# A hybrid decoder layer on one core: half-array products queued side by side, the first tiles multiplied by feature halves, a new order in the mixer

## The chip, the cores and the metric

One core of a Trainium2 chip runs one launch of the whole layer. The metric is the device time of that launch in microseconds (us), the median of several runs. The engines are TensorE (PE in the profile; PEld is its load of weights, which overlaps PE), VectorE (DVE), ScalarE (ACT), GpSimd (POOL) and SyncE (SP), whose queue issues nearly all DMAs here.

## The reference

All arithmetic is float32, with 512 tokens of 1024 features:

```python
h = swiglu(rms_norm(x, ffn1_pre_norm), w_gate, w_up, w_down)       # hidden width 2816
x = x + 0.5 * rms_norm(h, ffn1_post_norm)
u = rms_norm(x, mix_pre_norm)                                      # then u @ w_in, split in columns
o_nsa = g0 * o_cmp + g1 * o_sel + g2 * o_win                       # sparse attention: 8 heads of 64 in 2 groups
o_dn  = rms_norm(gated_delta_rule(q, k, v, decay, beta)) * silu(z) # gated DeltaNet: 4 heads of 128
o_mem = memory_cross_attention(mem_q, mem)                         # 4 heads of 128, 256 memory tokens
merged = sum(sigmoid(u @ w_branch_gate[br]) * (o[br] @ w_branch[br]) for br in range(3))
x = x + rms_norm(merged @ w_out, mix_post_norm)
h = swiglu(rms_norm(x, ffn2_pre_norm), w_gate, w_up, w_down)
x = x + 0.5 * rms_norm(h, ffn2_post_norm)
```

Two inner parts matter here. The compressed keys and values of the sparse attention come from a small network, `silu(flat @ w1) @ w2`, over blocks of 32 tokens (`flat` is 2048 wide, `w1` is 2048 x 256, one for keys and one for values). And each attention branch ends in the product of probabilities and values.

## The kernel before

Large products run with three matmuls for one: each operand is split into a high part of reduced precision (fp32r) and the rest, and high x high, low x high and high x low are summed (`mm3`, L117 to L119). `wload` (L105 to L109) brings a weight tile of 128 x 512 by a DMA on SP, ScalarE makes the high part, and VectorE (or, for every n-th tile of a task that says so, GpSimd) the low part. The tiles go round a small ring of buffers (tag `wraw`). Small products run in plain float32, where each matmul shows as two records in the trace.

A planner sets the order of the work. `tasks` (L1122) walks a list of short names and emits each task's instructions in that order. `off` raises the priority of a task's instructions by so many places. A scheduler then lays out each engine's queue from these priorities and a model of when operands are ready; on the chip each queue runs in order. `order(later, earlier)` tells the scheduler to place one instruction behind another, with no semaphore of its own. The lists and numbers are in the table `PRM` (L37): `order_s` for the start, `order0` for the first down-projection, `order` for DeltaNet and compression, `order2` for sparse attention, memory attention and merging, `order3` for the output projection.

**Start.** Eight bf16 matmuls on zeros run first. The order of the tasks is

```
t00 w10 w00 y t01 t02 w01 t03 w11 R0 F000 x F101 n F200 t10 t11 t12 t13 c F110 B F211 F011
```

`t0k` transposes two of the eight feature tiles of the first 256 tokens; `y` loads the second half of those tokens' features (the first half is loaded ahead of the list); `x` loads the other 256 tokens; `w10` loads half of the first up weights, `w00` half of the first gate weights; `F f i` multiplies hidden tile f for token half i: 48 matmuls of 256 columns, 24 for the gate and 24 for the up part, each over all 8 feature tiles.

**Compression (tasks p0 to p7, `cmp_hid`, L928).** Each of the 8 calls loads two weight tiles of 256 KB, one for keys and one for values, from the shared ring, and makes 4 products, which alternate between keys (array columns and PSUM partitions 0 to 63) and values (64 to 127). In the trace the result is `phid`, the line L940.

**Sparse attention.** For head i, branch br and group g, task `S` makes scores and softmax (L1042 to L1051), `P` transposes the probabilities tile by tile (`nsa_pt`, L1062) and copies them out, and `V` multiplies with the values (`nsa_pv`, L1074): 8 products per call, for g = 0 in array columns 0 to 63 and for g = 1 in 64 to 127, of 512, 384, 256 and 128 columns. There are 8 calls. `M br j` are the merge's tiles, 36 matmuls of 512 columns each. Others that are named below: `c` convolution of DeltaNet (projection, then `cacc`), `h` its transposes and norms, `k`, `l` its small products (`pkk`), `b`, `e`, `d` the inverse of its triangular blocks (`pt`, `px`, `pxt`), `s` its states, `o` its output, `q` the query projections, `x` the input of compression, `K` the keys.

Of the kernel before, what the change touches and what calls it, by code (L numbers as in the profile page):

```python
# [36 lines left out]
PRM = {'order': ['i', 'a', 'w', 'c01', 'h01', 'r0', 'c00', 'c10', 'c02', 'l0', 'h00', 'h02', 'c12', 'k0', 'h10', 'c22', 'c11', 'h12', 'h11', 'h22', 'r1', 'k1', 'l1', 'b0', 'c21', 'z', 'h21', 'e0', 'c20', 'r2', 'h20', 'c32', 'l2', 'c31', 'd00', 'h31', 'k2', 'r3', 'd01', 'l3', 'b1', 'd02', 'x0', 's00', 'e1', 'd10', 'c30', 'h32', 'x1', 'd11', 'h30', 's01', 's02', 's03', 'q0', 'q3', 'p0', 'o0', 'p1', 'p2', 'p3', 'k3', 'd12', 's10', 'p4', 'q1', 'p5', 's11', 'p6', 'p7', 's12', 's13', 'o1', 'q2', 'f'], 'dma': {'l': 'sync', 'b': 'sync', 'd': 'scalar', 'c': 'sync', 'r': 'sync'}, 'off': {'b0': 300, 'h31': 400, 'r1': 50, 'h32': 50, 'h11': 200, 'h12': 200, 'd10': 100, 'A01': 100, 'A10': 100, 'A11': 100, 'A20': 400, 'A31': 100, 'A21': 20, 'x0': 20, 'x1': 20, 'L': 200, 'S310': 400, 'S001': 20, 'S311': 400, 'A30': 100, 'r0': 400, 'd02': 20, 's11': 100, 'V20': 400, 'l3': 100, 'q1': 20, 'f': 400, 'l1': 20, 'h20': 100, 'h22': 100, 'r3': 50, 'P010': 50, 'y': 100, 'h02': 50, 'S101': 20, 'A00': 100, 'Q0': 50, 'Q1': 200, 'Q2': 50, 'Q3': 50, 'P110': 400, 'V31': 50, 'd01': 200, 'o0': 400, 'p0': 50, 'p1': 50, 'p2': 50, 'p4': 50, 'p5': 20, 'p6': 50, 'p7': 50, 'b1': 200, 'h01': 100, 'M15': 20, 'P201': 400, 'e0': 100, 'e1': 100, 'o1': 20, 'q0': 50, 'q2': 20, 'h21': 20, 'd11': 50, 'p3': 50, 'U0': 100, 's13': 50, 'c11': 20, 's00': 200, 'P011': 400, 'M14': 200, 'c20': 50, 'k2': 20, 'M03': 20}, 'ph': 'e', 'po': 'ss', 'xpd': (0, 1, 2), 'order2': ['K1', 'K0', 'B', 'M10', 'Q0', 'C0', 'Q1', 'S000', 'C3', 'S001', 'P001', 'P000', 'C1', 'S010', 'C2', 'S011', 'V00', 'P010', 'Q2', 'S101', 'S100', 'P011', 'S110', 'V01', 'P100', 'W0', 'P101', 'S111', 'Q3', 'V10', 'P110', 'M12', 'S200', 'P111', 'V11', 'P200', 'S210', 'M14', 'S201', 'M15', 'P201', 'S211', 'W1', 'V20', 'P211', 'P210', 'V21', 'S301', 'S300', 'W2', 'P301', 'S311', 'M11', 'P300', 'L', 'M13', 'S310', 'G0', 'V30', 'P310', 'M16', 'G2', 'P311', 'M17', 'V31', 'W3', 'A00', 'M00', 'A01', 'G1', 'U0', 'M05', 'A10', 'A11', 'G3', 'A30', 'U1', 'A31', 'U3', 'M03', 'M06', 'A20', 'A21', 'U2', 'M07', 'M22', 'M20', 'M02', 'M24', 'M27', 'M21', 'M23', 'M01', 'M04', 'M26', 'M25'], 'order0': ['d0', 'p0', 'n0', 't0', 'd1', 'k2', 'k0', 'p2', 'p3', 'v', 'k3', 'n1', 'k1', 't1'], 'order3': ['s3', 's7', 's2', 's6', 's1', 's5', 's0', 's4', 'd00', 'd01', 'd11', 'g', 'p0', 'n0', 't0', 'd10', 'p1', 'n1'], 't3': (('mm', 'r'), ('e', 's')), 'pool': {'W2': 2, 's13': 3, 'k0': 0, 'k1': 0, 'k2': 0, 'k3': 2, 'p3': 1, 'C0': 1, 'C1': 0, 'C2': 0, 'C3': 2, 'S310': 0, 'L': 3, 'd11': 3, 'p0': 1, 'p1': 1, 'p2': 1, 'p4': 2, 'p5': 1, 'p6': 1, 'p7': 1, 'S311': 0, 'h01': 0, 'h00': 2, 'h02': 0, 'h10': 0, 'h11': 0, 'h12': 0, 'h22': 0, 'h21': 0, 'h20': 0, 'h31': 0, 'h30': 3, 'h32': 0, 'i': 2, 'P011': 2, 'c21': 0, 'd01': 2, 'S000': 0, 'S001': 0, 'S010': 0, 'S011': 0, 'S100': 0, 'S101': 0, 'S110': 0, 'S111': 0, 'S200': 0, 'S201': 0, 'S210': 0, 'S211': 0, 'S300': 0, 'S301': 0, 'M24': 2, 'G2': 2, 'A01': 0, 'M10': 1, 'M15': 2, 'M12': 2, 'M14': 2, 'M13': 2, 'M17': 2, 'M11': 2, 'M16': 2, 'M23': 0, 'M27': 3, 'M01': 2, 'M00': 2, 'M03': 0, 'M07': 2, 'M06': 1, 'M22': 2, 'M04': 2, 'M20': 2, 'M26': 3, 'M02': 0, 'M21': 2, 'M25': 2, 'M05': 2, 'c11': 1, 'o1': 3, 'P000': 2, 'P001': 1, 'P010': 2, 'P100': 2, 'P101': 2, 'P110': 2, 'P111': 2, 'P200': 2, 'P201': 2, 'P210': 2, 'P211': 2, 'P301': 0, 'P300': 2, 'P310': 2, 'P311': 2, 'c12': 0, 'b1': 1, 'x0': 0, 'x1': 0, 'V21': 0, 'c30': 0, 'c01': 0, 'c02': 0, 'c00': 0, 'c10': 0, 'c22': 0, 'c20': 0, 'c31': 0, 'c32': 0, 's01': 3, 'A31': 0, 'd12': 0, 'y': 2, 'G0': 2, 'G1': 2, 'G3': 0, 'U3': 0, 'W3': 2, 'r1': 2, 's12': 3, 'U2': 0, 'Q0': 2, 'Q1': 2, 'Q2': 2, 'Q3': 1, 's00': 3, 's02': 2, 's03': 3, 's10': 2, 's11': 3, 'e1': 2, 'd00': 1, 'U0': 0, 'U1': 0, 'l2': 0, 'd02': 2, 'K1': 3, 'V11': 0, 'V00': 2}, 'pool3': {'d00': 3, 'd01': 3, 'd10': 3, 'd11': 0, 'p1': 2, 't1': 3, 't0': 3, 's5': 2, 's7': 2, 's1': 2, 's0': 2, 's3': 2, 's6': 2, 's2': 2, 's4': 2, 'q0': 1}, 'pool0': {}, 'off0': {'p3': 20, 'n1': 50, 'd0': 200, 'k2': 400, 'k1': 400}, 'off3': {'s1': 20, 's5': 200, 'g': 200, 't0': 400, 'd10': 200, 'p0': 200}, 'tt': ('e', 's'), 'order_s': ['t00', 'w10', 'w00', 'y', 't01', 't02', 'w01', 't03', 'w11', 'R0', 'F000', 'x', 'F101', 'n', 'F200', 't10', 't11', 't12', 't13', 'c', 'F110', 'B', 'F211', 'F011'], 't0': ('e', 's'), 'rs': ((0, 0), (0, 0)), 'ra': (1, 1), 'warm': 8, 'pools': {'F000': 0, 'F101': 0, 'F200': 0, 'F011': 0, 'F110': 0, 'F211': 0, 'w10': 0, 'w11': 0, 't00': 0, 't01': 0, 't02': 0, 't03': 0, 't13': 0, 't10': 0, 't11': 0, 't12': 0, 'w00': 0, 'w01': 0}, 'ptc': 'vvs', 'cva': 'v', 'offs': {'t13': 100, 'R1': 400, 't03': 20, 'w10': 200}, 'vnc': 's', 'sp3': 0, 'hsc': 'vv', 'sf2': 2, 'psc': 'vvvv', 'sp1': 0, 'vbs': 'v', 't1c': 'vs', 'sgv': 256}  # L37


class Body:  # L40
# [172 lines left out]
    def scale(self, eng, out, src, r):  # L213
        if eng == "s":
            self.nc.scalar.activation(out, src, AF.Copy, scale=r)
        else:
            (self.nc.gpsimd if eng == "g" else self.nc.vector).tensor_scalar(out, src, r, None, op0=OP.mult)
# [709 lines left out]
    def cmp_hid(self, c, Xs, d):  # L927

        nc = self.nc
        if c == 0:  # L930
            d["ph"] = self.bank(PRM.get("ph", "e"), "phid")[:, :256]
        w1 = []
        for which in range(2):
            w = self.wp.tile([P, 2, 256], F32, tag="wraw", name="w1", bufs=self.WB[0])
            nc.sync.dma_start(w, self.a["cmp_w1"][which, c])
            w1.append(w)
        for k in range(2):
            m = 2 * c + k
            for which in range(2):
                nc.tensor.matmul(d["ph"][64 * which : 64 * which + 64], Xs[which][:, m].rearrange("p g c -> p (g c)"),  # L940
                                 w1[which][:, k], start=m == 0, stop=m == 15)
# [89 lines left out]
    def nsa_soft(self, i, g, br, A, K, tb, sg, ap_):  # L1031
# [16 lines left out]
        for qb in range(TB):  # L1048
            n = P * (qb + 1)
            pm = Pm[:, self.OFF[qb] : self.OFF[qb] + n]  # L1050
            self.scale(PRM.get("psc", "vvvv")[qb], pm, pm, sm[:, qb : qb + 1])  # L1051
        return Pm

    def nsa_pt(self, Pm, ap_):
        nc, v, te = self.nc, self.nc.vector, self.nc.tensor
        PT = ap_.tile([P, 1280], F32, tag="PT", name="PT", bufs=2)
        for bank, kbs in enumerate(((0,), (1, 3), (2,))):
            pt = self.bank("s", "ppt")
            o = 0
# [8 lines left out]
    def nsa_pv(self, i, br, po, pts, vt):
        te = self.nc.tensor
        col = (0, 512, 1024, 896)  # L1070
        for kb in range(TB):
            n = SEQ - kb * P
            for g in range(2):
                te.matmul(po[64 * g : 64 * g + 64, kb * P :], vt[:, kb, br * P + 64 * g : br * P + 64 * g + 64],  # L1074
                          pts[g][:, col[kb] : col[kb] + n], start=br == 0 and kb == 0, stop=False, skip_group_check=True)
# [51 lines left out]
    def run(self):  # L1127
# [3 lines left out]
        with tc.tile_pool(name="f1", bufs=1) as fp, contextlib.ExitStack() as x1:  # L1131
# [384 lines left out]
```

## Time and profile before

| | |
|---|---|
| median of 3 runs (lowest, highest) | 1361.38 us (1360.89, 1362.07) |
| the profiled execution's own time | 1360.6 us |
| its span, first to last instruction | 1358.8 us |
| mean granted clock of TensorE | 0.995 |
| DMA traffic | 178.32 MB, mean 131 GB/s |
| matmul records on PE | 7839 |

The stages lie so in the span: the first feed-forward block to about 345 us, DeltaNet and compression from there to some 640, sparse attention and the merge to some 985, the output projection and the second feed-forward block after that.

In a row of the timeline stand the start and the duration in us, engine, line, operation, output and inputs, the shape (rows*columns of the array, then the output), the number of records, and in brackets the idle time before it and what ended it. Matmuls are pipelined: a record's duration runs past the start of the next one, so what an instruction costs the queue is the distance between starts. In a table by stretch, each engine has its busy time and, in brackets, its number of instructions. A row of waits has who waited for what, the total, how often, and the longest.

### The profile page before, as it was taken

Reading aid. Unit: us, or ns where it says so; the run is one execution under the profiler, and the core shown is the slowest. Engines: PE = TensorE matmul, PEld = TensorE weight load, DVE = VectorE, ACT = ScalarE, POOL = GpSimd, SP = SyncE. Lnnn points to the kernel's source line nnn. Section 1 sums busy time; section 2 is a strip of 40 time slices with the busy share of each in tenths; the row PEclk is TensorE's granted clock in tenths of the full one; section 3 lists DMA queues with packets and bytes.
Section 4 is the critical chain, followed back from the end, with each engine's and each line's share of the span. In section 5 each row is a group of like instructions: output and inputs, shape, how many; then the busy total and the mean of one; then the engine's idle time right before and its main releaser. Section 6 shows DMA issues by size and latency. Waiting matters only on the chain.

```text
span 1358.8 us, 21802 instructions
## 1 busy us (share of the span) xinstructions
PE 1330.2 (98%) x7839; PEld 1128.1 (83%) x7839; DVE 899.9 (66%) x1802; ACT 717.7 (53%) x1538; POOL 142.3 (10%) x129
## 2 busy tenths in 40 slices
PE   8999999999999989999999999999999999999997
PEld 7889999788797778787767777788878899998886
DVE  6897876765768775745887323322688778766775
ACT  6566664765655543316655234333576566646652
POOL 0020000000011322003111112323200000000000
PEclk8999999999999999999999999999999999999999
DMA  7543331586664341423111222533744433317773
GB/s 246 194 149 118 100 119 32 178 255 184 210 187 131 83 124 41 126 95 120 52 47 48 78 62 68 189 95 92 257 139 140 135 122 98 121 33 255 199 223 106
DMA packets 107453, 178.32 MB, mean 131 GB/s; under 512 B 18908, under 2 KB 28496, under 8 KB 107344
## 3 DMA queue, kind: packets, MB, share of 16 engines
q1 hardware_dynamic: 107056, 176.67, 41.9%
q8 instruction: 61, 1.00, 0.3%
q14 instruction: 48, 0.39, 0.1%
q10 hardware_dynamic: 288, 0.26, 0.1%
HBM read 166.84 MB, written 10.01 MB: 130 GB/s over the span
## 4 chain that ended last, share of the span: by engine, by line
PE 88%; DVE 5%; ACT 2%; DMA 2%; issue 1%; POOL 0%; SPq 0%; ACTq 0%; DVEq 0%; POOLq 0%
PE smm L429 10%; PE pfm L117 7%; PE pfm L118 7%; PE pfm L119 7%; PE se L429 7%; PE ss L429 3%; PE po L1074 2%; PE ps L1042 2%; PE acc_e L118 2%; PE acc_e L119 2%; PE acc_e L117 2%; PE sr L429 2%; PE acc_s L119 1%; PE acc_s L117 1%; PE acc_s L118 1%; PE so L429 1%
## 5 line engine op out<-in xcount | busy, mean ns | idle before, releaser
L106 ACT CAST whi<-wraw 128x512 fp32r<-128x512 f32 (+1 forms) x314 | 189.8, 614 | 181.4 <-PE pfm L119 65.1
L109 DVE TENSOR_TENSOR wlo<-wraw,whi 128x512 fp32r<-128x512 f32 (+1 forms) x268 | 183.9, 694 | 125.3 <-ACT whi L106 118.2
L117 PE MATMUL pfm<-xth,whi 128*128 128x512 f32 x384 | 154.5, 405 | 3.0 <-DVE cacc L635 3.0
L118 PE MATMUL pfm<-xth,wlo 128*128 128x512 f32 x384 | 154.2, 405 | 1.0 <-POOL wlo L109 1.0
L119 PE MATMUL pfm<-xtl,whi 128*128 128x512 f32 x384 | 154.5, 405 | 0.0
L117 PEld LDWEIGHTS pfm<-xth,whi 128*128 128x128 f32 x384 | 72.4, 189 | 21.0 <-issue 5.2
L119 PEld LDWEIGHTS pfm<-xtl,whi 128*128 128x128 f32 x384 | 72.4, 188 | 16.3 <-issue 2.0
L118 PEld LDWEIGHTS pfm<-xth,wlo 128*128 128x128 f32 x384 | 72.5, 189 | 16.1 <-POOL wlo L109 1.3
L109 POOL TENSOR_TENSOR wlo<-wraw,whi 128x512 fp32r<-128x512 f32 (+1 forms) x43 | 53.6, 1248 | 221.4 <-ACT whi L106 195.2
L106 ACT CAST ringh<-ringr 128x512 fp32r<-128x512 f32 x82 | 50.1, 620 | 42.8 <-PE acc_e L118 8.4
L429 PE MATMUL smm<-thi,fset 128*128 128x256 f32 x384 | 69.4, 279 | 0.0
L109 DVE TENSOR_TENSOR wlo<-ringr,ringh 128x512 fp32r<-128x512 f32 x75 | 51.3, 689 | 21.2 <-PE acc_e L119 6.8
L429 PEld LDWEIGHTS smm<-thi,fset 128*128 128x128 f32 x384 | 58.5, 188 | 0.2
L445 DVE TENSOR_TENSOR up<-smm,s 128x256 f32<-128x256 f32 x32 | 13.6, 424 | 66.5 <-ACT se L442 66.5
L429 PE MATMUL smm<-thi,fxtl 128*128 128x256 f32 x192 | 53.5, 279 | 0.6 <-DVE fxtl L411 0.6
L429 PE MATMUL smm<-thi,fxth 128*128 128x256 f32 x192 | 53.3, 277 | 0.0
L429 PE MATMUL se<-thi,fset 128*128 128x256 f32 x256 | 46.7, 280 | 0.0
L1045 ACT ACTIVATE Pm<-Pm,nm 128x128 f32<-128x128 f32 (+1 forms) x64 | 35.7, 559 | 15.5 <-DVE nm L1044 14.6
L402 DVE TENSOR_TENSOR fs<-fq 128x1024 f32<-128x1024 f32 x32 | 39.0, 1217 | 0.3 <-DMA fq<-in_ffn_u_dram 0.3
L429 PEld LDWEIGHTS se<-thi,fset 128*128 128x128 f32 x256 | 39.1, 187 | 0.0
L123 DVE TENSOR_TENSOR Hl<-H,Hh 128x256 fp32r<-128x256 f32 x88 | 34.9, 420 | 5.6 <-ACT Hh L122 3.7
L1044 DVE CUSTOM_DVE_ANT_0 Pm<-ps,tbl 128x128 f32<-128x128 f32 (+1 forms) x64 | 29.7, 484 | 10.9 <-PE ps L1042 10.3
(565 smaller groups left out, 3946.5 us busy)
## 6 DMA issues: line engine op xcount, KB each, us to landing
wraw<-in_ffn_d_dram SPq DMA_DIRECT2D x94, 256.0 KB, 2.8
ringr<-in_ffn_d_dram SPq DMA_DIRECT2D x82, 256.0 KB, 3.0
fq<-in_ffn_g_dram SPq DMA_DIRECT2D x64, 256.0 KB, 2.8
fq<-in_ffn_u_dram SPq DMA_DIRECT2D x64, 256.0 KB, 2.6
wraw<-in_w_gate_dram SPq DMA_DIRECT2D x48, 256.0 KB, 2.7
wraw<-in_ffn_u_dram SPq DMA_DIRECT2D x34, 256.0 KB, 3.2
wraw<-in_ffn_g_dram SPq DMA_DIRECT2D x34, 256.0 KB, 2.9
woraw<-in_w_out_dram SPq DMA_DIRECT2D x32, 256.0 KB, 3.0
```

Source lines behind the costliest of these rows:

```text
L106: nc.scalar.copy(hi, raw)
L109: eng.tensor_tensor(lo, raw, hi.bitcast(F32), op=OP.subtract)
L117: t.matmul(out, lh, rh, start=first, stop=False)
L118: t.matmul(out, ll, rh, start=False, stop=False)
L119: t.matmul(out, lh, rl, start=False, stop=last)
L123: return self.nc.vector.tensor_tensor(lo, src, hi.bitcast(F32), op=OP.subtract)
L402: add = lambda *x: v.tensor_tensor(*x, op=OP.add)
L429: m = lambda x, y, **kw: te.matmul(out, x, y, skip_group_check=True, **kw)
L1042: te.matmul(s[:, : max(n, 256)], A[:, qb * P : qb * P + P], K[j][:, : max(n, 256)], start=j == 0, stop=j == 1)
L1044: v.tensor_tensor_reduce(pm, s[:, :n], tb[:, SEQ - n :], -1.0, 3e38, op0=OP.add, op1=OP.min, accum_out=nm[:, qb : qb + 1])
L1045: nc.scalar.activation(pm, pm, AF.Exp, bias=nm[:, qb : qb + 1], scale=-1.0, accum_out=sm[:, qb : qb + 1])
L1074: te.matmul(po[64 * g : 64 * g + 64, kb * P :], vt[:, kb, br * P + 64 * g : br * P + 64 * g + 64], pts[g][:, col[kb] : col[kb] + n], start ...
```

## The change

1. `cmp_hid`: the weights of one call, for keys and values, come with one load of 512 KB into a tile with two buffers of its own (`w1` in the pool `cm`), no longer through the shared ring; the host lays them out to fit. The products and their order are the same.
2. `nsa_pv`: the first product of a call (kb = 0, g = 0) is ordered behind the last copy of the transposed probabilities of both groups.
3. `nsa_pt`: the first transpose is ordered behind the last scaling of the probabilities.
4. Start: tiles 0 and 1 of the first 256 tokens are multiplied by feature halves. A new task `P f c` makes the products of tile f over feature tiles 4c to 4c+3, up before gate; `w f i c` loads the weights for it. `F000` and `F101` then hold only what follows the products. The list becomes

```
t00 w010 w000 t01 P00 w110 y w100 P10 t02 w011 w001 t03 P01 w111 w101 R0 F000 P11 x n t10 F200 t11 F101 t12 t13 F110 B F211 F011 c
```

The first weight load has lost its raised priority (200), `w001` gets 100.

5. Orders. In `order`, c11 comes ahead of c22; b0, e0 and z come behind h21; k2 comes earlier, and so does d12; s01 goes ahead of h30; q0 goes from ahead of p0 to behind p1. Priorities: p1 to p7 go from 20 or 50 to 400; V00, V01, V10, V11, V21 and V30 get 400 and V31 goes from 50 to 400 (V20 has it before); smaller ones on h00, l2, h11, l1, i, P101, S210, G0, G2. In `order2` some S, P, C, M and W move by a few places, P000 ahead of P001. In `order0` d0 loses its 200, p0 gets 400, p2 100, and k1 goes from 400 to 20. In `order3` the splits start with s2, and d10 comes ahead of n0 and t0. For c12, r2, l3, M10, M26 and P300 the share of low parts that GpSimd makes changes.

```diff
     def nsa_pt(self, Pm, ap_):
+        Pm, after = Pm
...
-                    te.transpose(pt[:, o : o + P], ...)
+                    q = te.transpose(pt[:, o : o + P], ...)
+                    if not bank and not o and PRM.get("gp", 1):
+                        self.order(q, after)
...
-            (nc.scalar.copy if PRM.get("ptc", "svs")[bank] == "s" else v.tensor_copy)(dst, pt[:, :o])
-        return PT
+            q = (nc.scalar.copy if PRM.get("ptc", "svs")[bank] == "s" else v.tensor_copy)(dst, pt[:, :o])
+        return PT, q

     def nsa_pv(self, i, br, po, pts, vt):
...
+                if not kb and not g and PRM.get("gv", 1):
+                    for p in pts:
+                        self.order(q, p[1])

     def cmp_hid(self, c, Xs, d):
...
-        w1 = []
-        for which in range(2):
-            w = self.wp.tile([P, 2, 256], F32, tag="wraw", name="w1", bufs=self.WB[0])
-            nc.sync.dma_start(w, self.a["cmp_w1"][which, c])
-            w1.append(w)
+        w1 = d["cm"].tile([P, 2, 2, 256], F32, tag="w1", name="w1", bufs=2)
+        nc.sync.dma_start(w1, self.a["cmp_w1"][c])
...
-                                 w1[which][:, k], start=m == 0, stop=m == 15)
+                                 w1[:, k, which], start=m == 0, stop=m == 15)

+            def weights(f, i, c):
+                pre[f, i, c] = self.wload(a["ffn1_" + "gu"[i]][f][:, c * 512 : c * 512 + 512])
+
+            def half(f, c):
+                if c == 0:
+                    early[f] = [self.bank(t, "p" + n)[:, :256] for t, n in zip((("mm", "mm"), ("o", "r"))[f], "gu")]
+                for i in (1, 0):
+                    w = pre.pop((f, i, c))
+                    for k in range(4 * c, 4 * c + 4):
+                        j = slice(k % 4 * P, k % 4 * P + P)
+                        self.mm3(early[f][i], w[0][:, j], w[1][:, j], xh[:, k, :256], xl[:, k, :256], k == 0, k == 7)
```

More of the change, by code (lines that the diff above doesn't have):

```diff
@@ L214, in scale @@
         if eng == "s":
[L215 removed]
+            return self.nc.scalar.activation(out, src, AF.Copy, scale=r)
         else:
[L217 removed]
+            return (self.nc.gpsimd if eng == "g" else self.nc.vector).tensor_scalar(out, src, r, None, op0=OP.mult)
     def rowscale(self, xs, tbs, RB, engs, tag, after=None):
@@ L1050, in nsa_soft @@
             pm = Pm[:, self.OFF[qb] : self.OFF[qb] + n]
-            self.scale(PRM.get("psc", "vvvv")[qb], pm, pm, sm[:, qb : qb + 1])
-        return Pm
+            q = self.scale(PRM.get("psc", "vvvv")[qb], pm, pm, sm[:, qb : qb + 1])
+        return Pm, q
     def nsa_pt(self, Pm, ap_):
         nc, v, te = self.nc, self.nc.vector, self.nc.tensor
+        Pm, after = Pm
         PT = ap_.tile([P, 1280], F32, tag="PT", name="PT", bufs=2)
@@ L1073, in nsa_pv @@
             for g in range(2):
-                te.matmul(po[64 * g : 64 * g + 64, kb * P :], vt[:, kb, br * P + 64 * g : br * P + 64 * g + 64],
-                          pts[g][:, col[kb] : col[kb] + n], start=br == 0 and kb == 0, stop=False, skip_group_check=True)
+                q = te.matmul(po[64 * g : 64 * g + 64, kb * P :], vt[:, kb, br * P + 64 * g : br * P + 64 * g + 64],
+                              pts[g][0][:, col[kb] : col[kb] + n], start=br == 0 and kb == 0, stop=False, skip_group_check=True)
+                if not kb and not g and PRM.get("gv", 1):
+                    for p in pts:
+                        self.order(q, p[1])
     def mem_soft(self, h, pr, mq, kT, PT, ap_):
@@ L1135, in run @@
             H = fp.tile([P, FT, SEQ], F32, name="H")
-            pre, last, mark = {0: [], 1: []}, {}, {}
+            pre, last, mark, early = {}, {}, {}, {}
             def feat(i, k):
@@ L1150, in run @@
                 "t": feat,
-                "w": lambda i, c: pre[i].append(self.wload(a["ffn1_" + "gu"[i]][0][:, c * 512 : c * 512 + 512])),
+                "w": weights, "P": half,
                 "x": lambda: self.load_x(a["x"], x, last[0][0], tbs=(2, 3)),
@@ L1236, in run @@
             with tc.tile_pool(name="cm", bufs=1) as cmp_, tc.tile_pool(name="da", bufs=1) as self.da, tc.tile_pool(name="dn", bufs=1) as dp:
-                st, ys, Xs, R, E, sc = [{} for _ in range(4)], {}, {}, [{}, {}], {}, []
+                st, ys, Xs, R, E, sc = [{} for _ in range(4)], {}, {}, [{}, {}], {"cm": cmp_}, []
                 def small():
```

13 lines of the change are left out of this document (7 added, 6 removed).

## The prediction, made before the changed kernel was built

> **What bounds the kernel now.** I read the page first (engines and the chain that ended last), then a table by stage, then the two groups of instructions that the change regroups, one by one in the timeline, then who waited for whom, and last the first 20 us. From the page, busy time and the chain:
>
> ```profile
> PE 1330.2 (98%) x7839; PEld 1128.1 (83%) x7839; DVE 899.9 (66%) x1802; ACT 717.7 (53%) x1538; POOL 142.3 (10%) x129
> ...
> PE 88%; DVE 5%; ACT 2%; DMA 2%; issue 1%; POOL 0%; SPq 0%; ACTq 0%; DVEq 0%; POOLq 0%
> ```
>
> TensorE is the bound: 98% busy and 88% of the chain. So a change pays if it takes time out of TensorE's own queue, or out of the few waits in it. One row of the table by stage (busy time of PE, PEld, DVE, ACT, POOL, then clock and DMA), for the sparse attention:
>
> ```profile
> 640.00:745.00 105.00, 105.00 (x572) 75.41 (x571) 85.81 (x284) 59.83 (x172) 15.40 (x12) 1.00 0.19 60
> ```
>
> There PE never rests, and VectorE, next in line, has 105 - 85.8 = 19 us to spare. A busy PE is not a well used one, though. The products of probabilities and values (nsa_pv, L1074) fill only 64 of the array's 128 columns each. The table of those alone has one row for each of the eight calls (the first, the fifth and the sum stand here):
>
> ```profile
> 661.00:667.70 6.70, 3.87 (x16) 1.27 (x16) 1.00 0.15 42
> ...
> 720.00:723.00 3.00, 2.37 (x16) 1.06 (x16) 1.00 0.05 5
> ...
> sum 44.70, PE 25.61 PEld 9.67; mean PE 3.20 PEld 1.21
> ```
>
> The same 16 records take 3.87 us in one call and 2.37 in another. The timeline shows why:
>
> ```profile
> 661.07 1.07 PE L1074 MATMUL po<-PT,big 128*64 128x512 f32 x2
> ...
> 666.92 0.39 PE L1042 MATMUL ps<-KL,qa 128*128 128x512 f32 x1
> 667.24 0.43 PE L1074 MATMUL po<-PT,big 128*64 128x128 f32 x2
> 667.60 0.50 PE L119 MATMUL pfm<-xtl,whi 128*128 128x512 f32 x1
> 667.94 0.39 PE L117 MATMUL pfm<-xth,whi 128*128 128x512 f32 x1
> 668.16 0.40 PE L118 MATMUL pfm<-xth,wlo 128*128 128x512 f32 x1
> ...
> 781.18 1.52 PE L1074 MATMUL po<-PT,big 128*64 128x384 f32 x12
> ```
>
> The slow calls are torn: g=0 goes first without its partner g=1, then other work comes between. The eight calls lie in 19 pieces, of which the first and the last stand above; the fast ones are one piece of 16. A piece has a second price: the full-width product ahead of one holds the queue 0.32 us (666.92 to 667.24) and the one behind it 0.34 (667.60 to 667.94), where its like takes 0.22 (667.94 to 668.16). So entering costs 0.10 us and leaving 0.12.
>
> The compression's hidden product (cmp_hid, L940) has the same fault. First its group between 555 and 602 us, then the timeline:
>
> ```profile
> L940 PE MATMUL phid<-w,X 128*64 128x256 f32 x64 | 13.1, 397 | 0.3 <-DMA w<-in_cmp_w_dram 0.3
> ```
>
> ```profile
> 563.01 1.08 PE L940 MATMUL phid<-w,X 128*64 128x256 f32 x6
> ...
> 575.72 0.65 PE L940 MATMUL phid<-w,X 128*64 128x256 f32 x2
> 576.30 0.49 PE L119 MATMUL pfm<-xtl,whi 128*128 128x512 f32 x1
> ...
> 589.90 0.65 PE L940 MATMUL phid<-w,X 128*64 128x256 f32 x4
> 590.48 1.10 PE L791 MATMUL px<-T,DT 128*128 128x64 f32 x8
> ...
> 599.36 1.08 PE L940 MATMUL phid<-w,X 128*64 128x256 f32 x6
> ```
>
> Two records alone hold the queue 0.58 us (575.72 to 576.30), four together also 0.58 (589.90 to 590.48): the second half of the array comes free. The 64 lie in 15 pieces, from the first row to the last.
>
> **The change part by part.** *Attention products.* The first product of a call is ordered behind the last copy of both transposed tiles, and all eight calls get a priority of 400. If that makes every call one piece: 8 x 2.37 = 18.96 us, 6.65 less than 25.61. A piece's busy time runs 0.07 us into the next instruction (667.24 + 0.43 against 667.60), so 11 pieces fewer make 5.9 us of queue; 11 x 0.22 for entering and leaving adds 2.4: 8.3 us. Only the order on PE changes; no copy or product is added. PE's queue is in order, so what stands behind a product that waits for a late copy waits too: that cover is the full-width merge products now mixed in. With VectorE at 85.8 of some 97 us (105 - 8.3) instead of 105 a little will leak; I take 7.0.
>
> The transposes, ordered behind the last scaling, only close ranks: their narrow records pay nothing for neighbours of full width, and the copies behind them (VectorE) come at most a few tenths later. I cost it at nothing; without cover it would be part of the leak above.
>
> *Hidden product.* One load of 512 KB brings the weights for both halves, in two buffers of its own, so the eight records of a call (four products) become ready together. A call then takes at most 2 x 0.58 = 1.16 us, and at the rate of a whole attention call (4 x (512 + 384 + 256 + 128) = 5120 columns in 2.37 - 0.07 = 2.30 us) its 2048 columns take at least 0.92. I take 1.05, since the first pair of a piece is the dear one: 8.4 us against 13.1 - 15 x 0.07 = 12.1, so 3.7, and 7 pieces fewer at 0.22 make 1.5: 5.2 us. But at priority 400 these calls stop filling holes among DeltaNet's short dependent products (px, pxt), so I take 3.5.
>
> Who waits there now, on PE (400 to 660 us) and on the load queue (480 to 612), and what a load takes:
>
> ```profile
> PE pfm L117 <- DVE cacc L635: 3.0, 1, 3.0
> PE ptk L678 <- DVE kn L671: 2.1, 2, 1.7
> PE pkk L722 <- POOL kbT L700: 1.3, 2, 0.8
> ```
>
> ```profile
> SPq L935 <- DVE wlo L109: 15.0, 3, 7.5
> SPq L935 <- PE phid L940: 12.8, 6, 6.0
> ```
>
> ```profile
> w<-in_cmp_w_dram SPq DMA_DIRECT2D x16, 256.0 KB, 3.1
> ```
>
> Today these loads share a ring with the other weights and hold SP while VectorE frees a slot (15.0 us). With their own buffers that coupling goes, and the wait for earlier hidden products (12.8) stays. PE does not wait for it today beyond 0.3 us, so nothing is credited.
>
> *Start.* PE and ACT, then clock and DMA by stretch:
>
> ```profile
> 5.92 1.25 PE L198 MATMUL ptr<-cst,xa 128*128 128x128 f32 x8 [1.14 <-DMA xa<-in_x_dram]
> 9.18 0.66 PE L198 MATMUL ptr<-cst,xa 128*128 128x128 f32 x2 [2.01 <-DMA xa<-in_x_dram]
> 9.49 0.56 PE L117 MATMUL pg<-xth,whi 128*128 128x256 f32 x1
> ```
>
> ```profile
> 8.41 0.62 ACT L106 CAST whi<-wraw 128x512 fp32r<-128x512 f32 x1 [0.33 <-DMA wraw<-in_ffn_g_dram]
> ```
>
> ```profile
> 8.30:15.00 6.70, 5.82 (x28) 5.85 (x29) 4.37 (x9) 4.40 (x9) 0.00 (x0) 0.50 1.01 385
> 15.20:20.00 4.80, 4.80 (x42) 4.80 (x42) 3.27 (x15) 4.80 (x11) 0.00 (x0) 1.00 0.55 178
> ```
>
> PE stands 2.01 us for the second half of x, with no product begun. In the new order the half products P00 and P10 need only the first half of x and stand ahead of those transposes. The price: the first weight load loses its place ahead of x. The second load's cast starts at 8.41 now, with 256 KB more ahead of it than the new first load will have; at 385 GB/s that is 0.7 us, so the new cast ends near 8.41 + 0.62 - 0.7 = 8.3 and products start 1.2 us sooner. If the load lands right behind x, which comes 0.7 sooner as well, it is 5.9 - 0.7 + 0.7 + 0.62 = 6.5, or 3.0 sooner. I take 2.0, between them, and that the ramp to full clock moves with it. Bounds: -0.6 (that cast now lies behind x) to 3.0 + 1.7 = 4.7 (the half-rate stretch halved too, below). No product is added: 2 tiles of 48 in either form. The granted clock is 0.50 from 8.3 to 15.0 and 1.00 after.
> The Trainium skill, "TensorE: Matmul & The Clock Gate", Part 1, says the full rate comes after one busy window of about 3.4 us, whose phase runs freely. The 5.6 us from the first product (9.49) to the full rate (some 15.1) agree with it only as parts of two windows; by that rule an earlier start may win one whole window, an estimate of 3.4 / 2 = 1.7 us, and the total would be 1347.2.
>
> *Orders.* The lists of the mixer, the out-projection and the first down-projection are re-set: convolutions c11 and c22 swap, b0, e0, k2, q0, d12 and s01 move, loads of weights moving with them on SP, and some subtractions change between VectorE and POOL. Work is conserved; only waits can change. No row prices the new order. The three rows of PE waits above, 6.4 us, are the size of what can vanish or appear; I take 0, with both ends at 4.4.
>
> Sum: 7.0 + 3.5 + 2.0 + 0 = 12.5 us. The profiled execution took 1360.6 us, 0.8 below the median of 1361.38; against the median 1348.9.
>
> **The rivals.** *The cover runs out.* PE's shorter queue meets VectorE and the DeltaNet chain: half of attention's gain stays (4.0), none of the hidden product's, 2.0 of the start: 1355.4. For it: 85.8 of 105 us of VectorE, and short products waiting on each other near 590. Against: PE has no wait at all from 640 to 745.
>
> *The clock comes sooner.* With products from 8 us on, the half-rate stretch of 6.70 us halves: 6.7 / 2 at half rate is worth 1.7 us, 1347.2. For it: the gap of 2.01 us at its head goes. Against: transposes from 5.92 did not keep the clock up.
> The Trainium skill, "TensorE: Matmul & The Clock Gate", Part 1, states its mechanism (the free-running window above).
>
> *The orders pay as well.* 4.4 us of the waits vanish: 1344.5; with the sooner clock 1342.8. For it: the waits are real idle time on the bounding engine. Against: VectorE's and POOL's chains behind them are not shortened.
>
> *It doesn't do what it says.* The scheduler still tears the calls, as a priority of 50 did with the last one (781.18); only the start pays: 1359.4. Against: the call at 720 is whole already.
>
> *Slower.* The hidden product's loads choke SP and PE. A load of 512 KB takes between 3.1 us and twice that; the third waits in the queue for the first call's products, and every weight load behind it waits along. If PE runs dry each time, four rounds of 6.2 us against 8.4 us of work are 16.4 us of idle time: 1361.4 - 9.0 + 16.4 = 1368.8. It decides once PE's new waits between 500 and 640 us pass 9.0 + 2.7 us. Against: PE waited 0.3 us for these loads so far, and the projections q0 to q2 lie between the calls.
>
> **How the numbers follow.** 0.2% is 2.7 us, about what a measurement of this kernel can tell from no change. Forecast 0.45, clock sooner 0.15, cover runs out 0.18, orders pay 0.10, not done 0.06, slower 0.06. The first four are faster: 0.88; not done is the same: 0.06; slower 0.06. The range goes from under the case where orders and clock pay, 1341, to past the one where the cover runs out, 1358; it leaves out the last two cases and a little at the low end.
>
> **What would show it.** Eight rows of 2.3 to 2.4 us for the attention products and eight pieces in their timeline; the hidden product's group near 9 us; PE's first product before 8.5 us and a stretch at clock 0.50 that ends sooner; PE waits of the three kinds above still near 6.4 us. The prediction is wrong if the calls are whole and the span doesn't follow (then waits have come up between 545 and 790), or if PE waits for loads of the hidden product's weights.

## The result, and the profile after

The changed kernel takes 1344.07 us (median of 4 runs, 1343.02 to 1346.39); the kernel before took 1361.14 beside it (4 runs, 1359.14 to 1362.07). The ratio is 0.9879, with an interval of 0.9861 to 0.9897: 17 us less. The forecast was 1348.9, with a range of 1341 to 1358. So the direction and the range held, and the time came out 4.8 us below the forecast.

The profiled execution of the changed kernel took 1346.39 us, with a span of 1344.6. First its page, busy times and the chain that ended last:

```profile
PE 1316.8 (98%) x7839; PEld 1124.6 (84%) x7839; DVE 904.3 (67%) x1805; ACT 713.2 (53%) x1536; POOL 139.5 (10%) x126
...
PE 85%; DVE 6%; DMA 4%; ACT 2%; issue 2%; SPq 1%; POOL 0%; DVEq 0%; ACTq 0%
```

TensorE executes the same 7839 records, is 13.4 us less busy (1330.2 before), and is still the bound at 98%. Span and busy time fell together (14.2 and 13.4 us): the gain is TensorE's own time, and hardly idle time that went.

The products of probabilities and values (now L1075), one row for each of the eight calls, with PE and PEld busy time, clock, DMA share and GB/s:

```profile
654.00:657.50 3.50, 2.38 (x16) 1.09 (x16) 1.00 0.44 138
667.00:670.50 3.50, 2.38 (x16) 1.06 (x16) 1.00 0.01 2
680.50:684.00 3.50, 2.37 (x16) 1.06 (x16) 1.00 0.20 46
692.50:696.00 3.50, 2.38 (x16) 1.05 (x16) 1.00 0.14 34
707.00:710.00 3.00, 2.37 (x16) 1.06 (x16) 1.00 0.00 0
718.50:722.00 3.50, 2.37 (x16) 1.06 (x16) 1.00 0.23 75
733.50:737.00 3.50, 2.37 (x16) 1.06 (x16) 1.00 0.11 39
774.50:778.00 3.50, 2.37 (x16) 1.06 (x16) 1.00 0.27 80
sum 27.50, PE 18.99 PEld 8.50; mean PE 2.37 PEld 1.06
```

All eight are whole: 16 records in 2.37 or 2.38 us each, where before one call took 3.87, and the sum fell from 25.61 to 18.99. Around the first one, the timeline:

```profile
654.38 0.36 PE L1039 MATMUL ps<-KH,qa 128*128 128x256 f32 x1
654.68 2.38 PE L1075 MATMUL po<-PT,big 128*64 128x512 f32 x16
656.98 0.33 PE L995 MATMUL pct<-cst,cs 128*128 128x128 f32 x1
```

The call holds the queue from 654.68 to 656.98, 2.30 us. In what follows, the *queue time* of a group is the sum of such distances between starts, and a *piece* is a run of its records with nothing else between. By that count the eight calls went from 24.29 us in 19 pieces to 18.43 us in 8.

The compression's hidden product (now L937), its group between 555 and 602 us, and its first and last rows in the timeline:

```profile
L937 PE MATMUL phid<-w,X 128*64 128x256 f32 x64 | 8.5, 390 | 0.8 <-DMA w<-in_cmp_w_dram 0.7
```

```profile
562.41 1.95 PE L937 MATMUL phid<-w,X 128*64 128x256 f32 x16
...
582.77 1.08 PE L937 MATMUL phid<-w,X 128*64 128x256 f32 x8
583.78 0.43 PE L784 MATMUL pt<-Dm,LT 128*128 128x64 f32 x2
```

8.5 us busy against 13.1, and 7 pieces against 15 (the first row is two calls side by side); its queue time went from 12.0 to 7.96 us. A whole call of eight records holds the queue 1.01 us (582.77 to 583.78). PE waits 0.7 us for one of the new loads.

The start, PE's rows:

```profile
7.70 0.38 PE L117 MATMUL pu<-xth,whi 128*128 128x256 f32 x1 [0.64 <-ACT whi L106]
8.71 0.39 PE L117 MATMUL pg<-xth,whi 128*128 128x256 f32 x1 [0.62 <-ACT whi L106]
```

The first product begins at 7.70 instead of 9.49, and PE's waits beside it are for the first casts of weights (0.64 and 0.62 us) instead of 2.01 us for the second half of x. PE's waits between 400 and 660 us, with total, count and longest:

```profile
PE ptk L678 <- DVE qs L671: 2.7, 2, 1.6
PE ptk L678 <- DVE kn L671: 1.8, 1, 1.8
PE ptk L678 <- DVE Bi L744: 1.4, 1, 1.4
PE pfm L117 <- ACT whi L106: 1.0, 1, 1.0
PE phid L937 <- DMA w<-in_cmp_w_dram: 0.7, 1, 0.7
PE pfm L118 <- DVE wlo L109: 0.6, 1, 0.6
PE pkk L722 <- POOL kbT L700: 0.6, 1, 0.6
PE pot L847 <- DVE on L846: 0.3, 1, 0.3
PE pfm L117 <- DVE cacc L635: 0.3, 1, 0.3
```

The 3.0 us for cacc are 0.3 now, but waits for qs and Bi have come up. The same view of before adds up to 8.9 us, of which the prediction showed the upper 6.4; after it is 9.4, and 9.8 with two rows of 0.2. So in this stage waits are no source of the gain. From 633 to 800 us PE waits for nothing (the kernel before waits 1.0 us at 636 us for a weight and for nothing from 640 to 790), though VectorE works 77.97 of the first 95 us:

```profile
633.00:728.00 95.00, 95.00 (x544) 71.45 (x544) 77.97 (x262) 55.52 (x160) 15.58 (x12) 1.00 0.19 56
```

Where the 14.2 us of span went, by landmarks of the two traces: 1.95 us by the first record of line L429 in the first feed-forward block (70.98 to 69.04), 4.0 by the 2,500th record on PE, shortly behind that block (392.68 to 388.69), 7.2 by the first score product of the attention (644.78 to 637.57), 15.4 by the end of the last product into `po` (794.46 to 779.09); the rest of the kernel gives back 1.2. So about 2 us came at the start, 2 in the rest of the first feed-forward block and behind it, 3 in DeltaNet and compression, 8 in the attention. The second 2 us were in no sum: a wait of PE of 1.1 us, at 352 us for `xa`, is gone. Which of the re-set priorities ended it is not shown. These are two single executions, and the first 2 us hang on the clock as well, as the part on the prediction shows.

The transposes of the probabilities changed too, though the prediction put them at nothing. Their queue time went from 16.14 us in 48 pieces to 15.08 in 43. And a product behind a piece of them is dearer, here in the changed kernel:

```profile
659.17 0.38 PE L1061 MATMUL ppt<-cst,Pm 128*128 128x128 f32 x2
659.30 0.48 PE L117 MATMUL pfm<-xth,whi 128*128 128x512 f32 x1
659.62 0.39 PE L118 MATMUL pfm<-xth,wlo 128*128 128x512 f32 x1
659.85 0.39 PE L119 MATMUL pfm<-xtl,whi 128*128 128x512 f32 x1
```

The first product holds the queue 0.32 us (659.30 to 659.62), the next one 0.23. At 0.09 a piece, 5 pieces fewer make 0.4, so the transposes are worth an estimated 1.5 us.

### The profile page after: what moved, and what is told of

Its sections match the earlier page's. It is cut to its first block, busy times and chain, and to the rows that moved or that the text cites. A ratio compares the mean times of both kernels' runs of the same rounds, so it can differ in the third digit from the quotient of the medians.

```text
span 1344.6 us, 21791 instructions
## 1 busy us (share of the span) xinstructions
PE 1316.8 (98%) x7839; PEld 1124.6 (84%) x7839; DVE 904.3 (67%) x1805; ACT 713.2 (53%) x1536; POOL 139.5 (10%) x126
## 4 chain that ended last, share of the span: by engine, by line
PE 85%; DVE 6%; DMA 4%; ACT 2%; issue 2%; SPq 1%; POOL 0%; DVEq 0%; ACTq 0%
PE smm L429 10%; PE pfm L117 7%; PE pfm L118 7%; PE pfm L119 7%; PE se L429 7%; PE ss L429 3%; PE acc_s L119 2%; PE acc_s L117 2%; PE acc_s L118 2%; PE ps L1039 2%; PE sr L429 2%; PE so L429 1%; PE acc_e L118 1%; DVE wlo L109 1%; PE acc_e L119 1%
## 5 line engine op out<-in xcount | busy, mean ns | idle before, releaser
L109 DVE TENSOR_TENSOR wlo<-wraw,whi 128x512 fp32r<-128x512 f32 (+1 forms) x271 | 188.7, 704 | 108.4 <-ACT whi L106 103.4
L109 POOL TENSOR_TENSOR wlo<-wraw,whi 128x512 fp32r<-128x512 f32 (+1 forms) x40 | 49.9, 1247 | 191.2 <-ACT whi L106 178.4
L429 PE MATMUL smm<-thi,fset 128*128 128x256 f32 x384 | 69.4, 279 | 0.0
L429 PEld LDWEIGHTS smm<-thi,fset 128*128 128x128 f32 x384 | 58.5, 188 | 0.2
L429 PE MATMUL smm<-thi,fxtl 128*128 128x256 f32 x192 | 53.5, 279 | 0.6 <-DVE fxtl L411 0.6
L429 PE MATMUL smm<-thi,fxth 128*128 128x256 f32 x192 | 53.3, 277 | 0.0
L429 PE MATMUL se<-thi,fset 128*128 128x256 f32 x256 | 46.7, 280 | 0.0
L1042 ACT ACTIVATE Pm<-Pm,nm 128x128 f32<-128x128 f32 (+1 forms) x64 | 35.6, 558 | 14.2 <-DVE nm L1041 13.8
L429 PEld LDWEIGHTS se<-thi,fset 128*128 128x128 f32 x256 | 39.1, 187 | 0.0
L429 PEld LDWEIGHTS smm<-thi,fxtl 128*128 128x128 f32 x192 | 36.1, 188 | 1.0 <-DVE fxtl L411 1.0
```

The source lines that it names most:

```text
L109: eng.tensor_tensor(lo, raw, hi.bitcast(F32), op=OP.subtract)
L429: m = lambda x, y, **kw: te.matmul(out, x, y, skip_group_check=True, **kw)
L1042: nc.scalar.activation(pm, pm, AF.Exp, bias=nm[:, qb : qb + 1], scale=-1.0, accum_out=sm[:, qb : qb + 1])
```

## The experiments

The theory: the two halves of the array run side by side when their records are neighbours in PE's queue, and each piece costs a further 0.22 us at its edges (the prediction's figure); a variant's time follows that sum. The rivals: the new lists carry the gain by themselves (other waits); or it is the start and its clock; or the halves don't matter and it is only the number of pieces. Each kernel was measured beside the kernel before. The new order at the output projection was not run alone. A ratio is given with its 95% interval; differences in us are differences of ratios, times 1361.

### Parts alone, put into the kernel before

**Attention's edges and priorities alone** (b_pv).

```diff
 # nsa_pt, nsa_pv: both order() edges of the change
-'V31': 50
+'V00': 400, 'V01': 400, 'V10': 400, 'V11': 400, 'V21': 400, 'V30': 400, 'V31': 400
```

> The kernel before, with the attention part alone: both ordering edges and a priority of 400 on all eight calls of the attention product. Theory A (a part is worth the queue time that it takes out of TensorE): eight pieces of 2.3 us, 24.3 - 18.4 = 5.9 us of slots plus about 2 us of entering and leaving, so 7 to 8 us faster. Theory B (the new orders are what lets the saving through; alone it turns into waits): 4 us or less, with new PE waits between 640 and 790 us.

Measured: 1358.21 us (11 runs), ratio 0.9984 (0.9974 to 0.9993): 2.2 us, not 7 or 8. The calls are only partly mended: 20.87 us of queue in 13 pieces.

**Hidden product alone** (b_hid).

```diff
-w = self.wp.tile([P, 2, 256], F32, tag="wraw", name="w1", bufs=self.WB[0])      # two loads
+w1 = d["cm"].tile([P, 2, 2, 256], F32, tag="w1", name="w1", bufs=2)             # one load
-'p1': 50, 'p2': 50, 'p3': 50, 'p4': 50, 'p5': 20, 'p6': 50, 'p7': 50
+'p1': 400, 'p2': 400, 'p3': 400, 'p4': 400, 'p5': 400, 'p6': 400, 'p7': 400
```

> The kernel before, with the hidden product's part alone: one load of 512 KB in two buffers of its own, priority 400 on p1 to p7. Theory A: 12.0 - 8.0 = 4.0 us of slots and 1.5 us of entering and leaving, so 5 us faster. Theory B (these products were filling holes among DeltaNet's small dependent products): 0 to 2 us, and PE waits between 540 and 640 us grow by 3 us or more.

Measured: 1360.54 us (11 runs), ratio 1.0 (0.9987 to 1.0012): nothing. Yet its queue time fell from 12.0 us in 15 pieces to 9.5 in 9, worth 2.5 + 6 x 0.22 = 3.8 us. PE's waits between 400 and 660 us of this kernel, the top two rows, show what took part of it back:

```profile
PE pfm L117 <- DVE cacc L635: 2.9, 1, 2.9
PE phid L937 <- DMA w<-in_cmp_w_dram: 2.6, 2, 2.1
```

PE waits 2.6 us for the new loads, 2.3 more than before. All rows of this view add up to 12.0 us, 3.1 more than the 8.9 of before. 3.8 - 3.1 leaves 0.7 us, which the interval (some 1.7 us on either side) does not tell from nothing.

**Start alone** (b_start): `order_s`, `pools`, `offs` and the functions `weights` and `half`.

```diff
-'order_s': ['t00', 'w10', 'w00', 'y', 't01', 't02', 'w01', ...]
+'order_s': ['t00', 'w010', 'w000', 't01', 'P00', 'w110', 'y', 'w100', 'P10', 't02', ...]
```

> The kernel before, with the start alone (tiles 0 and 1 by feature halves, the new order of loads). Theory A: the 1.95 us by which the fast phase began sooner in the changed kernel, all of it at the end: 2 us faster, with the half-rate stretch gone. Theory B (what is won at the start is lost to the loads after it): within 1 us of before.

Measured: 1360.49 us (11 runs), ratio 0.9996 (0.9987 to 1.0005). This does not tell 0 from 1.8 us.

**First down-projection's priorities alone** (b_down).

```diff
-'off0': {'p3': 20, 'n1': 50, 'd0': 200, 'k2': 400, 'k1': 400}
+'off0': {'p3': 20, 'n1': 50, 'k2': 400, 'k1': 20, 'p2': 100, 'p0': 400}
```

> The kernel before with the first down-projection's new priorities alone (d0 loses 200, p0 400, p2 100, k1 20). Theory A (moves waits only): within 1 us of before. Theory B (traces with these priorities reach the mixer some 2 us sooner after the fast phase): 2 us faster.

Measured: 1359.41 us (11 runs), ratio 0.9993 (0.9984 to 1.0002). Inconclusive: about 2 us at most.

**The mixer's lists alone** (b_mix): `order`, `order2`, `pool` and the small entries of `off`, without the priorities of V and p and without new code.

```diff
-'order2': [..., 'V00', 'P010', 'Q2', ..., 'Q3', 'V10', 'P110', 'M12', 'S200', ...]
+'order2': [..., 'P010', 'C2', 'S011', 'V00', 'Q2', ..., 'Q3', 'P110', 'S200', 'S210', 'V10', ...]
```

> The kernel before, with the mixer's new lists alone (order, order2, the smaller priorities, GpSimd's shares), without the priorities of the attention calls and of p1 to p7 and without the new code. Theory A (the lists only move waits about): within 3 us of before. Theory B (the lists carry the gain): 5 us or more faster. A third: they lose 2 to 5 us alone, since they were set for shorter products; that would explain why the mixer as a whole won 9.5 us and not 13.5.

Measured: 1372.08 us (5 runs), ratio 1.0076 (1.0063 to 1.0089): 10 us **slower**. One call in its timeline:

```profile
760.36 1.07 PE L1074 MATMUL po<-PT,big 128*64 128x512 f32 x2
761.37 0.49 PE L119 MATMUL pfm<-xtl,whi 128*128 128x512 f32 x1
761.79 1.07 PE L1074 MATMUL po<-PT,big 128*64 128x512 f32 x2
762.79 0.49 PE L117 MATMUL pfm<-xth,whi 128*128 128x512 f32 x1
...
768.43 0.43 PE L1074 MATMUL po<-PT,big 128*64 128x128 f32 x2
768.79 0.50 PE L117 MATMUL pfm<-xth,whi 128*128 128x512 f32 x1
```

The scheduler set one full-width merge product between every two products of the call (each is two records): eight lone products from 760.36 to 768.79. The merge product between holds the queue 0.42 us (761.37 to 761.79) instead of 0.22. In all, the calls lie in 29 pieces and take 28.95 us of queue, against 19 and 24.29 before. PE also waits 2.1 us between 640 and 790 us, where it waited for nothing before. The rival that the lists pay by themselves falls with this run.

**The lists, with attention's edges and priorities** (b_mixpv): b_mix plus the edit of b_pv.

> The kernel before, with the mixer's new lists and the attention part together (both edges, priority 400 on the eight calls), the old hidden product and the old start. Theory A (parts add): 10.3 slower for the lists, some 2.5 faster for the attention part, so about 1369. Theory B (lists and edges belong together: with the edges the lists' torn calls close, without them they tear): eight pieces of 2.3 us and some 8 to 11 us faster than before, so 1350 to 1353.

Measured: 1354.44 us (5 runs), ratio 0.9954 (0.9941 to 0.9966). The calls are whole (18.43 us, 8 pieces), as in the changed kernel. The same edit that was worth 2.2 us in the old lists is worth 16.6 in the new ones (1.0076 to 0.9954).

### The changed kernel, with one part undone

**Without the edge ahead of the first product of a call** (a_gv0).

```diff
+'gv': 0        # in nsa_pv: if not kb and not g and PRM.get("gv", 1): order(q, p[1])
```

> The changed kernel without the edge ahead of the attention product (its priority of 400 stays). If the edge is what keeps the halves together: the calls tear as with the lists alone (28.96 us in 29 pieces), 8 to 14 us slower, 1352 to 1358. If the priority does it: eight pieces, 1344.

Measured: 1354.66 us (5 runs), ratio 0.9955 (0.9941 to 0.9968): 10.3 us of the gain gone; 24.75 us of queue in 19 pieces. The priority alone doesn't do it.

**With the old priorities of V, edges kept** (a_vprio0).

```diff
-'V00': 400, 'V01': 400, 'V10': 400, 'V11': 400, 'V21': 400, 'V30': 400, 'V31': 400
+'V31': 50
```

> The changed kernel with the old priorities on the eight attention calls (V20 400, V31 50, none on the others), both edges kept. If the edges alone keep a call whole: eight pieces, 1344. If it takes both, as the edge took the priority before (13 pieces with the old lists): torn calls, 3 us slower or more.

Measured: 1360.01 us (11 runs), ratio 0.9996 (0.9987 to 1.0004): 15.9 us, nearly the whole gain, gone. Products with values between 600 and 900 us in this kernel:

```profile
600.00:900.00 300.00, 29.47 (x128) 9.89 (x128) 1.00 0.26 81
```

The same 128 records take 29.47 us, more than the 25.61 of before, in 27 pieces. The edge alone doesn't do it either: it sets when a call may begin, and the priority keeps others from being set in between.

**Whole calls, but the halves one after the other** (a_gouter). Each call is still one piece of 16 records; only the two loops are exchanged, so that g = 0 comes first with all its columns. The edge stands ahead of the first product of each half.

```diff
-for kb in range(TB):
-    for g in range(2):
+for g in range(2):
+    for kb in range(TB):
...
-                if not kb and not g and PRM.get("gv", 1):
+                if not kb:
```

> The changed kernel with the eight products of an attention call in another order: all four of g = 0, then all four of g = 1 (same products, same result). Theory A (the gain is two halves of the array working at once): a call's slot goes from 2.3 to 4.4 to 5.0 us at the 0.9 to 1.0 ns a column of lone records, so 17 to 21 us slower, 1361 to 1365, with some of it hidden. Theory B (the gain is that a call is in one piece, whatever its order): within 2 us of 1344.

Measured: 1357.85 us (11 runs), ratio 0.9976 (0.9967 to 0.9985): 13.2 us of the gain gone. Its first call in the timeline:

```profile
655.61 0.36 PE L1039 MATMUL ps<-KH,qa 128*128 128x256 f32 x1
655.90 3.93 PE L1075 MATMUL po<-PT,big 128*64 128x512 f32 x16
659.76 0.33 PE L995 MATMUL pct<-cst,cs 128*128 128x128 f32 x1
```

The same neighbours on both sides, the same 16 records, no wait: 3.86 us of queue (655.90 to 659.76) against 2.30. Eight calls, 12.4 us more. This is the run that decides between the theory and the rival of the pieces: one piece is not enough, the two halves must alternate.

**With the old hidden product and the old priorities of p** (a_nohid): the edit of b_hid reversed.

> The changed kernel with the old hidden product: two loads of 256 KB through the shared ring, old priorities for p1 to p7. Theory A (worth as much as alone): no change, 1344. Theory B (with the new lists around it the part pays its queue time): 4 to 6 us slower than the changed kernel, 1348 to 1350.

Measured: 1352.56 us (5 runs), ratio 0.994 (0.9927 to 0.9952): 8.3 us gone. The queue gives 11.51 - 7.96 = 3.55 us and 9 pieces x 0.22 = 2.0, together 5.5. The wait for the weights is 0.9 longer (1.6 us against 0.7), but all of PE's waits from 400 to 660 us add up to 9.6, no more than the 9.8 of the changed kernel. In the profiled runs the stretch from the 2,500th record to the first score product is 4.0 us longer (252.9 against 248.9). The interval of the difference is some 3 us on either side, so the remaining 2.8 us may be nothing. The clock may have a part in it: in the profiled run of this kernel the start was at half clock from 7.5 to 14.3 us, in that of the changed kernel it was not, and with the same start the first record of line L429 begins 1.7 us later (70.71 against 69.04). What part is which stays open.

**With the old list of DeltaNet and compression** (a_oldorder): only `order` as before.

> The changed kernel with the old list for DeltaNet and compression (order), everything else as changed. Theory A (the lists only move waits: PE's waits from 395 to 660 us are 8.8 us before and 9.8 after): within 1 us of 1344. Theory B (the new list is what makes room for the hidden product and it ends the wait of 3.0 us for cacc, in which three traces lost a clock window of 3.4 us): 3 to 8 us slower, 1347 to 1352, with that wait back near 500 us.

Measured: 1349.69 us (5 runs), ratio 0.9926 (0.9913 to 0.9938): 6.4 us gone. Two of PE's waits, from 400 to 660 us:

```profile
PE pfm L117 <- DVE cacc L635: 3.0, 1, 3.0
...
PE phid L937 <- DMA w<-in_cmp_w_dram: 1.8, 1, 1.8
```

The wait for cacc is back (2.7 us more) and the wait for the hidden product's weights is 1.1 longer, but the waits for qs and Bi have gone: all rows add up to 10.7 us, 0.9 more than the 9.8 of the changed kernel. A stretch at half clock behind the first of these waits costs some 1.6 us (last section), and the hidden product lies in 9 pieces with 8.69 us (0.73 + 2 x 0.22 = 1.2). That makes 3.7 us, and in the profiled runs the stretch from the 2,500th record to the first score product grew by 4.0. Of the measured 6.4, with some 3 us on either side, the rest stays open.

**With the old start** (a_nostart): the edit of b_start reversed.

> The changed kernel with the old start (tiles 0 and 1 multiplied whole, the old order of loads). Theory A (the start is worth what its own milestone showed, the fast phase 1.6 to 1.95 us sooner): about 2 us slower than the changed kernel, 1346. Theory B (the start alone measured within noise, so it is nothing here too): 1344 to 1344.5.

Measured: 1345.64 us (4 runs), ratio 0.9893 (0.9879 to 0.9906), 1.9 us from the changed kernel's 0.9879, with intervals that overlap. By itself it doesn't show a gain.

### The sum of queue time and pieces, against the runs

| pair | queue, us | pieces x 0.22 | sum | measured |
|---|---|---|---|---|
| before to b_pv | -3.4 | -6: -1.3 | -4.7 | -2.2 |
| before to b_mix | +4.7 | +10: +2.2 | +6.9 | +10.3 |
| b_mix to b_mixpv | -10.5 | -21: -4.6 | -15.1 | -16.6 |
| changed kernel to a_gv0 | +6.3 | +11: +2.4 | +8.7 | +10.3 |
| changed kernel to a_vprio0 | +9.2 | +19: +4.2 | +13.3 | +15.9 |
| changed kernel to a_gouter | +12.4 | 0 | +12.4 | +13.2 |

The intervals are 1.3 us on either side in the first row, 1.8 in the second and 2.5 to 3 in the others. In the last four the sum follows, short by 0.8 to 2.6 us each time. It misses the first two, and there PE's waits between 640 and 790 us, of which the kernel before has none, take up a part. b_pv has 0.7 us of them, which brings 4.7 to 4.0, still more than its measured 0.9 to 3.5. b_mix has 2.1, which brings 6.9 to 9.0, inside its 8.6 to 12.1. What b_pv lost beyond that stays open. A half-clock stretch of 3.4 us stands at 506 us in its profiled run and not in that of the kernel before. But both have the wait that the last section ties it to, so it can't be counted against the edit. No run changes the number of pieces alone, so the 0.22 us a piece is tested only within these sums.

## Why the prediction was right, and where its sizes were off

**Attention products: right.** The 5.9 us of queue and the 11 pieces are what the trace has (24.29 - 18.43 = 5.86; 19 - 8 = 11), and a_gouter and a_gv0 show that pairing is the cause. The step that was too small is the discount: "a little will leak; I take 7.0". VectorE had 85.8 us of work for some 97, and PE still waits for nothing from 633 to 800 us. The whole 8.3 came. One reading beside it was wrong: that the transposes' "narrow records pay nothing for neighbours of full width". They pay nothing ahead of them, but the product behind takes 0.32 us instead of 0.23. So most of the 0.12 that the prediction charged for leaving a piece is not special to products on half of the array; what they alone pay is the entry, 0.10.

**Hidden product: right in kind, too small.** The step "so I take 3.5" took a third off 5.2 because the calls would no longer fill holes among DeltaNet's short products. Queue time and pieces gave 4.0 + 8 x 0.22 = 5.8 us, the waits in this stage took 0.9 of it (8.9 to 9.8), and leaving the part out cost 8.3 +- 3. The landmarks show less, 3.2 us for the whole stage (4.0 to 7.2), so its size is good to some 2 us at best. A whole call takes 1.01 us where 1.05 was assumed.

**Start: the products came sooner, but the 2.0 us are not shown.** The first product begins at 7.1 to 7.7 us in the seven profiled kernels with the new start and at 8.9 to 9.7 in the seven with the old one, 1.9 us sooner in the mean, as forecast. What failed is the step from there to 2.0 us of the total, "and that the ramp to full clock moves with it". At the first record of line L429, near 70 us, the new starts stand at 68.8 to 71.2 us (mean 69.7) and the old ones at 69.8 to 71.0 (mean 70.4): 0.6 us are left, less than the spread of either group. The 1.95 us between the two main traces are in large part the clock of these two executions. b_start (0.5 us by its median) and a_nostart (1.9) do not settle it either. The changed kernel in the timeline, then a_nostart (old start), then a_nohid (new start) in a table by stretch:

```profile
8.93 0.27 PE L118 MATMUL pu<-xth,wlo 128*128 128x256 f32 x1
9.04 0.28 PE L119 MATMUL pu<-xtl,whi 128*128 128x256 f32 x1
```

```profile
13.34 0.41 PE L118 MATMUL pg<-xth,wlo 128*128 128x256 f32 x1
13.55 0.41 PE L119 MATMUL pg<-xtl,whi 128*128 128x256 f32 x1
```

```profile
8.20:14.20 6.00, 5.82 (x28) 5.76 (x27) 2.62 (x5) 2.41 (x5) 0.00 (x0) 0.50 0.84 312
14.40:20.00 5.60, 5.60 (x50) 5.60 (x49) 4.25 (x8) 5.11 (x12) 0.82 (x1) 1.00 0.81 273
```

A product of 256 columns holds the queue 0.21 us at half clock (13.34 to 13.55) and 0.11 at full clock (8.93 to 9.04). The changed kernel is at full clock from 7.0 us, ahead of its first product; a_nohid, with the same start, is at half clock from 7.5 to 14.3 us. In the profiled runs the full clock comes to stay between 7.0 and 14.6 us with the new start (7 kernels, mean 11.7) and between 11.6 and 15.1 with the old one (7 kernels, mean 13.3). The Trainium skill, "TensorE: Matmul & The Clock Gate", Part 1, says that its window of about 3.4 us runs freely and that the change to full clock therefore varies by 500 ns either way; here kernels with the same start differ by up to 7.6 us (7.0 to 14.6). In six of these seven traces a stretch at half clock of 3.4 or 6.8 us begins between 7.5 and 8.5 us; in the changed kernel's there is none. So "the clock comes sooner" happened in the profiled run, where the full clock came at 7.0 instead of 15.1, but no run ties it to the new start: a mean granted clock of 0.999 stands in 13 of 52 runs of kernels with the new start and in 16 of 110 with the old.

It does enter the measured number. All four runs of the changed kernel have 0.999; the 63 runs of the kernel before beside the experiments have 0.993 (5 runs, mean 1363.31 us) to 0.999 (7 runs, mean 1359.45). Against those seven the gain is 1359.45 - 1344.39 (the mean of the four) = 15.1 us. Whether the changed kernel has the full clock more often than others, or four runs were lucky, stays open.

**Orders: the step that failed.** "Work is conserved; only waits can change; I take 0." The waits did about cancel, as assumed: cacc's wait went, others came. But the work of PE is not conserved under a new order. How long these products hold the queue depends on what stands between them, and that is what the lists, priorities and edges decide together. Alone, the lists cost 10.3 us (b_mix); alone, edges and priorities gave 2.2, the hidden product 0, the start 0.5 by its median. These four make 7.6 us slower, and together (with small changes at the two projections) they are 16.5 us faster. So the parts of the mixer's change have no price of their own: the sum in the prediction came out near because it priced the end state (every call whole), not because its parts can be added. The old `order` put back in the end state costs 6.4 us, so "orders pay" was true as well, but in part by the hidden product and by a clock window behind the wait that the rival named.

**The account.** Attention 8.3, hidden product 5.8, transposes 1.5 and the wait for `xa` 1.1, less 0.9 for the waits between 400 and 660 us, make 15.8 us before anything for the start. Against it stand 17.1 between the medians (interval 14.0 to 18.9), 15.1 at like clock and 14.2 between the spans of the two profiled executions. So the sum agrees with the two large terms, and the small ones, the start among them, can't be told apart by it. That 12.5 fell in the range was owed in part to errors that lay on both sides: attention and hidden product too small by 3.6 us, the transposes and the wait for `xa` left out, the start probably too large.

**The rivals.** *The cover runs out* did not happen to the whole. Of the parts alone, b_hid gave nothing, as that rival has it; b_pv gave 2.2 us against its 4.0, but for another reason: its calls stayed in 13 pieces, with 0.7 us of new waits. *It doesn't do what it says* is a_vprio0 (0.9996): the edges without the priorities tear the calls as before. *Slower* asked for 16.4 us of waits for the hidden product's loads; there were 0.7 in the changed kernel, and 1.8 to 2.6 with the old list (a_oldorder and b_hid).

No kernel tried here beats the changed one.

## What to carry to other kernels

Where products fill half of the array, count their queue time from start to start and their pieces, not their busy time: 16 records held TensorE 2.30 us with the halves alternating and nothing between them, 3.86 with one half after the other, and as lone products between full-width ones the call stretched over 8.4 us (760.36 to 768.79), of which the seven others would need 1.5 by themselves. Tell the scheduler both when the group may begin (an edge behind its last operand) and that nothing comes between (a priority): here either one alone lost 10 to 16 us. And price such a change by its end state: an edit that looks worthless or harmful alone may be what the others need.

## What was not expected of the hardware

One wait of PE of 3.0 us was followed by a stretch at half clock, in five of the six profiled kernels that have it. The kernel a_oldorder in the timeline and in a table by stretch (clock third from the end), and the changed kernel, which has no such wait, in the same stretch:

```profile
505.11 0.47 PE L117 MATMUL pfm<-xth,whi 128*128 128x512 f32 x1 [3.00 <-DVE cacc L635]
...
507.32 0.63 PE L119 MATMUL pfm<-xtl,whi 128*128 128x512 f32 x1
507.74 0.63 PE L117 MATMUL pfm<-xth,whi 128*128 128x512 f32 x1
```

```profile
506.20:509.50 3.30, 3.30 (x11) 2.62 (x10) 2.36 (x6) 1.47 (x8) 0.00 (x0) 0.50 0.54 169
```

```profile
506.20:509.50 3.30, 3.30 (x16) 2.66 (x15) 2.98 (x7) 1.49 (x8) 0.00 (x0) 1.00 0.26 74
```

The same product goes from 0.23 us of queue to 0.42 (507.32 to 507.74) for 3.41 us. The kernel before and b_pv, b_start and b_hid have the same instructions there. From the product behind the wait to the hundredth record after it, the kernel before takes 15.35 us, without the half clock, and these three 16.88 to 16.93: some 1.6 us lost on top of the wait. Six profiled kernels have this wait: five of them show the half clock (b_down for 6.8 us), the kernel before in its one profile does not; of the eight without the wait none does. The Trainium skill, "TensorE: Matmul & The Clock Gate", Part 1, gives one idle window of about 3.4 us as what lowers the clock; here a wait shorter than that was enough in five cases of six. So removing a wait near 3 us on TensorE can be worth half as much again.
